# First block of a column sum loaded by two transfers, 16 partitions and then 112, in place of one of 128

## The chip, the cores and the metric

The kernel runs on one core of a Trainium2 chip. The metric is the device time of one execution in microseconds (us), the median over runs.

## The reference

```
x = randn(8192, 8192).astype(float32)
def reference(x): return np.sum(x, axis=0)
```

The input is 268.4 MB, the output 32 KB. Every byte of x has to come into the core once.

## The kernel before

x is cut into 32 blocks of 256 rows. A block lies in SBUF, the core's on-chip memory, as 128 partitions with two rows each, that is 65,536 bytes in one piece per partition. In the trace each such piece is one packet of a DMA engine. Three buffers take turns. The SyncE queue (SP) issues one transfer per block, and VectorE adds two 8192-wide rows at a time into a running sum.

```
P = 128; K = 2; NBUF = 3
xr = x.rearrange("(b p k) c -> b p k c", p=P, k=K)
bufs = [pool.tile([P, K, C], F32, ...) for b in range(NBUF)]
...
def take(sem, n):
    nc.vector.sem_inc(sem, -n)._wait_ge(sem, n)
def block(b):                         # two additions per block
    take(s_buf[b], 17)                # 16 from the transfer, 1 from the block before
    ... tensor_tensor row 0 += carry            (L123)
    nc.vector.sem_inc(s_free, 1)                # the buffer of the block before is free
    ... tensor_tensor row 1 += row 0            (L128)
...
take(s_buf[0], 16)                    # block 0
nc.vector.tensor_tensor(out=rows(0, 1), in0=rows(0, 1), in1=rows(0, 0), op=ADD)   # L134
...
for t in range(last):
    i = nc.sync.dma_start(out=bufs[t % NBUF][:], in_=xr[t])
    if t >= NBUF:
        i._wait_ge(s_free, t - NBUF + 1)
    i.then_inc(s_buf[t % NBUF], 16)
```

The last block comes in six strips of columns. TensorE, with a matrix of ones, sums it and the carry over the partitions; that tail is not touched by the change.

## Time and profile before

| | before |
|---|---|
| time, median of 5 runs beside the change | 627.57 us (627.48 to 627.78) |
| share of the DMA engines' time | 99.2% |
| VectorE busy | 85% |
| rate in the steady part | 434 GB/s |
| first addition on VectorE starts at | 23.16 us |

The page's groups of instructions tell how VectorE stands to the DMA. The columns are: line, engine, operation, output and inputs by name and by shape, count, busy us, mean ns of one, then the idle time before them and what ended it (DVEq L118 is VectorE's own sequencer at the wait in `take`).

```profile
L123 DVE TENSOR_TENSOR buf<-buf,buf 128x8192 f32<-128x8192 f32 x29 | 252.1, 8693 | 58.2 <-DVEq L118 58.2
...
L134 DVE TENSOR_TENSOR buf<-buf 128x8192 f32<-128x8192 f32 x1 | 8.7, 8693 | 23.2 <-DVEq L118 23.2
```

VectorE waits 58.2 us before 29 blocks, 2 us each, and 23.2 us for the first one. It follows the DMA stream. The other views of the kernel before are read in the prediction.

### The profile page before, as it was taken

How to read it: one execution, taken by the hardware profiler on the slowest of the kernel's cores; microseconds unless marked ns; L12 is line 12 of the kernel's file. 1: busy time of each engine (PE TensorE's matmuls, PEld its weight loads, DVE VectorE, ACT ScalarE, POOL GpSimd, SP SyncE). 2: the span in 40 equal slices, each digit the busy share in tenths (PEclk: the TensorE clock that was granted, in tenths of full speed). 3: DMA queues.
4: the chain of work that ended last, by engine and by line, in shares of the span. 5: the costliest groups of instructions: out<-in, count | busy, mean ns of one | idle time of the engine just before them, and what ended most of it. 6: DMA issues, size and time to landing. Idle time of an engine off the chain costs nothing. (4 is left out here: it accounts for less than half of the span.)

```text
span 625.9 us, 576 instructions
## 1 busy us (share of the span) xinstructions
PE 14.2 (2%) x148; PEld 4.5 (1%) x148; DVE 530.8 (85%) x65; ACT 3.7 (1%) x6; POOL 0.3 (0%) x5
## 2 busy tenths in 40 slices
PE   0000000000000000000000000000000000000017
PEld 0000000000000000000000000000000000000002
DVE  0538988889888899888898888988889888899886
ACT  0000000000000000000000000000000000000001
POOL 0000000000000000000000000000000000000000
PEclk9999999999999999999999999999999999999999
DMA  9999999999999999999999999999999999999997
GB/s 402 402 469 402 465 406 465 406 465 406 457 415 436 436 415 457 402 469 402 469 402 469 402 469 402 469 402 465 406 461 410 452 419 431 440 410 461 402 429 312
DMA packets 6141, 268.49 MB, mean 429 GB/s; under 512 B 620, under 2 KB 880, under 8 KB 1404
## 3 DMA queue, kind: packets, MB, share of 16 engines
q1 hardware_dynamic: 6120, 268.47, 99.2%
q8 instruction: 1, 0.02, 0.0%
q10 hardware_dynamic: 20, 0.00, 0.0%
HBM read 268.44 MB, written 0.03 MB: 429 GB/s over the span
## 5 line engine op out<-in xcount | busy, mean ns | idle before, releaser
L123 DVE TENSOR_TENSOR buf<-buf,buf 128x8192 f32<-128x8192 f32 x29 | 252.1, 8693 | 58.2 <-DVEq L118 58.2
L128 DVE TENSOR_TENSOR buf<-buf 128x8192 f32<-128x8192 f32 x29 | 252.1, 8693 | 6.9 <-DVEq L118 6.9
L134 DVE TENSOR_TENSOR buf<-buf 128x8192 f32<-128x8192 f32 x1 | 8.7, 8693 | 23.2 <-DVEq L118 23.2
L85 PE MATMUL ps<-buf,ones 128*32 128x512 f32 (+3 forms) x144 | 12.6, 496 | 608.8 <-DMA buf<-in_x_dram 608.1
L72 DVE TENSOR_TENSOR buf<-buf,buf 128x4096 f32<-128x4096 f32 x2 | 8.8, 4422 | 1.6 <-DMA buf<-in_x_dram 1.6
L72 DVE TENSOR_TENSOR buf<-buf 128x2048 f32<-128x2048 f32 (+1 forms) x3 | 8.9, 3000 | 0.1
L85 PEld LDWEIGHTS ps<-buf,ones 128*32 128x32 f32 x144 | 4.1, 114 | 617.1 <-DMA buf<-in_x_dram 610.6
L209 ACT COPY res<-ps 128x512 f32<-128x512 f32 (+2 forms) x5 | 2.5, 491 | 618.5 <-PE ps L85 618.5
L209 DVE COPY res<-ps 128x64 f32<-128x64 f32 x1 | 0.2, 225 | 2.6 <-PE ps L85 2.6
L100 PE MATMUL ps<-buf,ones 128*32 128x512 f32 x4 | 1.9, 592 | 0.0
L209 ACT ACT_TABLE_LOAD x1 | 1.3, 1283 | 0.9 <-SPq L108 0.9
L100 PEld LDWEIGHTS ps<-buf,ones 128*32 128x32 f32 x4 | 0.4, 110 | 1.3 <-issue 1.3
L109 POOL MEMSET ones<- 128x32 f32 x1 | 0.1, 125 | 0.5 <-SPq L108 0.5
L256 POOL MEMSET const-bfloat16-1.0<- 128x1 bf16 x1 | 0.1, 102 | 0.0
L256 POOL MEMSET const-uint8-127<- 128x1 uint8 x1 | 0.1, 102 | 0.0
L256 POOL MEMSET const-float32-0.0<- 128x1 f32 x1 | 0.1, 99 | 0.2 <-issue 0.2
L256 POOL MEMSET const-float32-1.0<- 128x1 f32 x1 | 0.1, 99 | 0.0
## 6 DMA issues: line engine op xcount, KB each, us to landing
buf<-in_x_dram SPq DMA_DIRECT2D x3, 2048.0 KB, 19.4
buf<-in_x_dram SPq DMA_DIRECT2D x1, 1024.0 KB, 25.5
buf<-in_x_dram SPq DMA_DIRECT2D x1, 768.0 KB, 26.8
buf<-in_x_dram SPq DMA_DIRECT2D x31, 29.7
buf<-in_x_dram SPq DMA_DIRECT2D x1, 256.0 KB, 22.6
out_dram<-res SPq DMA_DIRECT2D x1, 24.0 KB
out_dram<-res SPq DMA_DIRECT2D x1, 4.0 KB
out_dram<-res ACTq DMA_DIRECT2D x1, 4.0 KB
```

Source lines behind the costliest of these rows:

```text
L72: i = nc.vector.tensor_tensor(out=o, in0=a, in1=b, op=ADD)
L85: i = nc.tensor.matmul(out=ps[n][32 * j : 32 * j + 32, 0 : w // NJ], lhsT=ones[:], rhs=runs[:, j], start=start, stop=True, skip_group_chec ...
L100: nc.tensor.matmul(out=ps[len(STRIPS)][0:32, :], lhsT=ones[:], rhs=rows(last, 1, 0, 512), start=True, stop=True,)
L109: nc.gpsimd.memset(ones[:], 1.0).then_inc(s_one, 1)
L123: nc.vector.tensor_tensor(out=r0, in0=r0, in1=bufs[(b - 1) % NBUF][:, 1, :], op=ADD).then_inc(s_op, 1)
L128: nc.vector.tensor_tensor(out=r1, in0=r1, in1=r0, op=ADD).then_inc(s_buf[(b + 1) % NBUF], 1)
L134: nc.vector.tensor_tensor(out=rows(0, 1), in0=rows(0, 1), in1=rows(0, 0), op=ADD).then_inc(s_buf[1], 1)
L209: c = nc.vector.tensor_copy(out=o, in_=p) if n == 5 else nc.scalar.copy(o, p)
L256: nc = _bacc.Bacc("TRN2", target_bir_lowering=False, num_devices=1)
```

## The change

Block 0 gets two transfers. The first has one partition for each of the 16 DMA engines, presumably so that every engine gets its first piece of work sooner. The second has the other 112 partitions. VectorE waits for both.

```diff
-        take(s_buf[0], 16)
+        take(s_buf[0], 32)
...
         for t in range(last):
+            if t == 0:
+                nc.sync.dma_start(out=bufs[0][0:16], in_=xr[0][0:16]).then_inc(
+                    s_buf[0], 16
+                )
+                nc.sync.dma_start(out=bufs[0][16:P], in_=xr[0][16:P]).then_inc(
+                    s_buf[0], 16
+                )
+                continue
             i = nc.sync.dma_start(out=bufs[t % NBUF][:], in_=xr[t])
```

## The prediction

> **What bounds the kernel now.** I read four views, in this order: the page's busy times and slices, its DMA part, the table of busy time by stage, and the timeline of the start. The page says at once which resource is full.
>
> ```profile
> span 625.9 us, 576 instructions
> PE 14.2 (2%) x148; PEld 4.5 (1%) x148; DVE 530.8 (85%) x65; ACT 3.7 (1%) x6; POOL 0.3 (0%) x5
> ...
> DMA  9999999999999999999999999999999999999997
> ...
> q1 hardware_dynamic: 6120, 268.47, 99.2%
> ```
>
> The reader is to see that the 16 DMA engines are busy in every slice (q1 took 99.2% of their time), while VectorE, the busiest compute engine, is at 85%. A kernel that reads 268.4 MB once and has its DMA engines full can only be made shorter before the first byte, after the last one, or by a faster stream. How fast the stream is, the stages show (last two columns: DMA share, GB/s):
>
> ```profile
> 0.00:23.20 23.20, 0.00 (x0) 0.00 (x0) 0.04 (x1) 1.28 (x1) 0.33 (x5) 1.00 0.97 407
> 23.20:42.40 19.20, 0.00 (x0) 0.00 (x0) 8.66 (x1) 0.00 (x0) 0.00 (x0) 1.00 1.01 437
> 42.40:592.40 550.00, 0.00 (x0) 0.00 (x0) 495.48 (x57) 0.00 (x0) 0.00 (x0) 1.00 1.00 434
> ```
>
> 434 GB/s over 550 us is 27.1 GB/s for each of 16 engines. A row of a block is 2 x 8192 x 4 = 65,536 B, one packet, so one packet takes 65,536 / 27.1 = 2.42 us; the packet records in the trace say 2.418. A block of 128 rows is 8 packets on each engine, 19.35 us. The start in half microseconds:
>
> ```profile
> 1.50:2.00 0.50, 0.00 (x0) 0.00 (x0) 0.00 (x0) 0.50 (x1) 0.00 (x0) 1.00 1.15 393
> 2.00:2.50 0.50, 0.00 (x0) 0.00 (x0) 0.00 (x0) 0.19 (x1) 0.00 (x0) 1.00 4.35 1442
> 2.50:3.00 0.50, 0.00 (x0) 0.00 (x0) 0.00 (x0) 0.00 (x0) 0.00 (x0) 1.00 0.75 262
> 3.00:4.50 1.50, 0.00 (x0) 0.00 (x0) 0.00 (x0) 0.00 (x0) 0.00 (x0) 1.00 0.00 0
> ```
>
> A packet is booked whole where it starts, so 393, 1442 and 262 GB/s in half a microsecond are 3, 11 and 2 packets: all 16 engines begin between about 2.0 and 2.65 us, each with one packet. The packet records give 2.9 to 3.4 us for these first ones (0.5 to 1.0 over the normal 2.42) and a spread of 0.65 us between the first and the last engine's start. No engine pauses afterwards. The timeline shows what the start does to VectorE:
>
> ```profile
> 0.97 70.02 SPq L167 DMA_DIRECT2D buf<-in_x_dram  x5
> 23.16 8.69 DVE L134 TENSOR_TENSOR buf<-buf 128x8192 f32<-128x8192 f32 x1 [23.16 <-DVEq L118]
> 42.45 8.69 DVE L123 TENSOR_TENSOR buf<-buf,buf 128x8192 f32<-128x8192 f32 x1 [10.60 <-DVEq L118]
> 51.38 8.69 DVE L128 TENSOR_TENSOR buf<-buf 128x8192 f32<-128x8192 f32 x1 [0.24 <-DVEq L118]
> 61.78 8.69 DVE L123 TENSOR_TENSOR buf<-buf,buf 128x8192 f32<-128x8192 f32 x1 [1.71 <-DVEq L118]
> ```
>
> The queue issues at 0.97 us, block 0 is added at 23.16, and the next two blocks follow 19.3 us apart, the pace of the DMA. VectorE needs 17.4 us a block and waits some 2 us for each. So VectorE would follow a late stream, and would not add to it.
>
> [...]
>
> **The change part by part.** It removes one issue of 8 MB and adds two, of 1 MB and 7 MB. VectorE waits for 32 instead of 16; no arithmetic, buffer or later transfer changes.
> (1) Issue: one more instruction on the queue, 0.33 us by the records of this line (327 to 432 ns). It runs while the first packets move, at 2.9 us or more each. Cost 0.
> (2) Completion: each engine has one more small packet, of 9 ns in the records, some 0.02 us with its gap. Cost 0.02.
> (3) Start, the intent as I read it: the short transfer may be dealt out sooner, so that the last engine need not begin 0.65 us after the first. The most it can save is that spread[...]. I put it at 0.3 us saved.
> (4) [...]
> (5) [...]
> (6) After that. An engine has 248 packets of full rows and then the strips, back to back[...]. The slowest is the last at the end too. A late landing moves VectorE and the later issues with it. Transfers wait in the queue some 10 us (29.7 us median from issue to landing against 19.4 of transfer), so an engine ahead of the others may run dry, but the slowest one does not.
> Sum: 0.02 - 0.3 + 15.3 = +15.0, so 627.5 + 15.0 = 642.5 us.
>
> **The rivals.**
> A, [...]only (1) to (3) act, and the time is 627.2, between 626.8 and 627.7. [...]Chance 0.11.
> B, [...]+7 to +10, so 635 to 637. Chance 0.22.
> C, [...] are consecutive: +12 to +20, 639.5 to 647.5. Chance 0.50.
> D, [...] are dealt in turn, row by row or four by four: [...]+58 us, 685; four by four gives about +39. Chance 0.17.
> A wait that takes the place of another I don't expect: the extra count comes from the transfer that now lands last anyway, and VectorE has its 2 us of slack a block.
>
> **Range and chances.** Two per cent is 12.55 us, so slower begins at 640.05 us, inside C near its lower part. Slower: about 0.8 of C and all of D, 0.57. Faster needs 615, which no path of the start can give, with 2 us before the first byte: 0.01. The rest, A, B and the low part of C, is 0.42. The range 627.0 to 657.0 leaves out D and the better part of nothing else; it is lopsided because a bad dealing of the rows has no near bound.
>
> **What would show it.** Right: packets of the first transfer at 9 to 10 us instead of 3, so few bytes between 3 and 10 us; the first addition at about 38 us instead of 23.16; packets of the second transfer at 2.4 to 7 us, unevenly; the steady 434 GB/s and 2.42 us from block 1 or 2 on; VectorE's 8.69 us per addition the same. Wrong: first packets of about 3 us say [...](A); a first addition at 31 to 33 us says B, after 60 us D. If the start is late by as much as I say but the end is not, the skew between engines was made up, which (6) denies.

The sum of the forecast came to +15.0 us, 642.5 us in all, with a range of 627.0 to 657.0. The 15.3 us in it were the figure for steps (4) and (5), the slower packets of the first and of the second transfer. Both steps, and parts of the rivals, rested on an assumption about which partitions slow each other when they are written at once, and no run had shown it. The rivals: A, the two transfers cost nothing; B and C, block 0 comes late, and in C each engine gets seven consecutive partitions of the 112; D, the 112 rows go out in turn. The figures of B, C and D rest on the same assumption.

## The result

The changed kernel took 649.07 us (median of 5 runs, 648.55 to 649.38), the kernel before 627.57 in the same rounds: 21.5 us more, a ratio of 1.0342 with a 95% interval of 1.0326 to 1.0357. Ratios here are the mean time of one kernel's fast runs over that of the other's of the same rounds, so they are not quite the ratio of the medians quoted.

The page of the changed kernel, its span, busy times, DMA slices and main queue:

```profile
span 647.6 us, 577 instructions
...
PE 14.2 (2%) x148; PEld 4.5 (1%) x148; DVE 530.8 (82%) x65; ACT 3.7 (1%) x6; POOL 0.3 (0%) x5
...
DMA  9999999999999999999999999999999999999986
...
q1 hardware_dynamic: 6136, 268.47, 99.1%
```

No engine has more work: VectorE is busy for 530.8 us as before. The DMA engines look as full as before, and that is the trap of this view: a packet that is slow counts as busy for all of its time. What they moved shows it: in the first stage below the share is 0.96 at 117 GB/s. The table of stages (last two columns: DMA share and GB/s; a packet is booked whole where it starts, so short stages are coarse):

```profile
0.00:9.00 9.00, 0.00 (x0) 0.00 (x0) 0.00 (x0) 1.28 (x1) 0.33 (x5) 1.00 0.96 117
9.00:18.40 9.40, 0.00 (x0) 0.00 (x0) 0.00 (x0) 0.00 (x0) 0.00 (x0) 1.00 1.09 223
18.40:44.00 25.60, 0.00 (x0) 0.00 (x0) 0.00 (x0) 0.00 (x0) 0.00 (x0) 1.00 0.94 241
44.00:60.00 16.00, 0.00 (x0) 0.00 (x0) 8.69 (x1) 0.00 (x0) 0.00 (x0) 1.00 1.05 455
60.00:610.00 550.00, 0.00 (x0) 0.00 (x0) 491.50 (x57) 0.00 (x0) 0.00 (x0) 1.00 1.00 433
```

For 44 us the stream runs at about a quarter, then about half of its rate; from the second block on it is what it was, 433 GB/s. The start, closer:

```profile
2.00:2.50 0.50, 0.00 (x0) 0.00 (x0) 0.00 (x0) 0.19 (x1) 0.00 (x0) 1.00 14.16 1704
2.50:3.00 0.50, 0.00 (x0) 0.00 (x0) 0.00 (x0) 0.00 (x0) 0.00 (x0) 1.00 3.11 393
3.00:4.50 1.50, 0.00 (x0) 0.00 (x0) 0.00 (x0) 0.00 (x0) 0.00 (x0) 1.00 0.00 0
...
10.00:11.00 1.00, 0.00 (x0) 0.00 (x0) 0.00 (x0) 0.00 (x0) 0.00 (x0) 1.00 2.14 393
11.00:12.00 1.00, 0.00 (x0) 0.00 (x0) 0.00 (x0) 0.00 (x0) 0.00 (x0) 1.00 2.99 590
```

13 and 3 packets start before 3 us, and most of the engines take up their second one only after 10 us. Before, all 16 second packets (699 GB/s in 1.5 us) started between 4.5 and 6 us:

```profile
4.50:6.00 1.50, 0.00 (x0) 0.00 (x0) 0.00 (x0) 0.00 (x0) 0.00 (x0) 1.00 1.61 699
```

The timeline of SP and VectorE in the changed kernel:

```profile
0.96 0.40 SPq L169 DMA_DIRECT2D buf<-in_x_dram  x1
1.43 0.40 SPq L172 DMA_DIRECT2D buf<-in_x_dram  x1
...
45.30 8.69 DVE L134 TENSOR_TENSOR buf<-buf 128x8192 f32<-128x8192 f32 x1 [45.30 <-DVEq L118]
64.58 8.69 DVE L123 TENSOR_TENSOR buf<-buf,buf 128x8192 f32<-128x8192 f32 x1 [10.58 <-DVEq L118]
```

The first addition starts at 45.30 us, 22.1 later than before; the next follows at the old distance of 19.3. And the groups:

```profile
L123 DVE TENSOR_TENSOR buf<-buf,buf 128x8192 f32<-128x8192 f32 x29 | 252.1, 8693 | 57.8 <-DVEq L118 57.8
...
L134 DVE TENSOR_TENSOR buf<-buf 128x8192 f32<-128x8192 f32 x1 | 8.7, 8693 | 45.3 <-DVEq L118 45.3
```

The whole loss is in the one wait for block 0; the other 29 waits are unchanged. So the question is only why block 0 takes 22 us longer to land.

The packet records answer it by the step. The records don't name the engine, but within 0.03 us of the end of each packet another one starts, so they can be strung into 16 rows of 248 packets, one for each engine. The mean of all first, all second packets and so on, in us:

| | 1st | 2nd | 3rd | 4th | 5th | 6th | 7th | 8th |
|---|---|---|---|---|---|---|---|---|
| before | 3.13 | 2.42 | 2.42 | 2.42 | 2.42 | 2.42 | 2.42 | 2.42 |
| changed | 8.63 | 5.47 | 4.76 | 3.33 | 3.84 | 4.64 | 4.76 | 4.61 |

The first column is the transfer of 16 partitions, the other seven are the 112. I had expected the first column. I had not expected that the others would be slow on nearly all engines alike (the third packets took 4.74 to 4.86 us, the seventh 4.72 to 4.83).

### The profile page after: what moved, and what is told of

Read it like the earlier page. It is cut to its first block, busy times and chain, and to the rows that moved or that the text cites. A ratio compares the mean times of both kernels' runs of the same rounds, so it can differ in the third digit from the quotient of the medians.

```text
span 647.6 us, 577 instructions
## 1 busy us (share of the span) xinstructions
PE 14.2 (2%) x148; PEld 4.5 (1%) x148; DVE 530.8 (82%) x65; ACT 3.7 (1%) x6; POOL 0.3 (0%) x5
## 5 line engine op out<-in xcount | busy, mean ns | idle before, releaser
L123 DVE TENSOR_TENSOR buf<-buf,buf 128x8192 f32<-128x8192 f32 x29 | 252.1, 8693 | 57.8 <-DVEq L118 57.8
L85 PEld LDWEIGHTS ps<-buf,ones 128*32 128x32 f32 x144 | 4.1, 115 | 638.8 <-DMA buf<-in_x_dram 632.3
```

What stands on the lines that cost most here:

```text
L85: i = nc.tensor.matmul(out=ps[n][32 * j : 32 * j + 32, 0 : w // NJ], lhsT=ones[:], rhs=runs[:, j], start=start, stop=True, skip_group_chec ...
L123: nc.vector.tensor_tensor(out=r0, in0=r0, in1=bufs[(b - 1) % NBUF][:, 1, :], op=ADD).then_inc(s_op, 1)
```

## The experiments

A step is here one row on each of the 16 engines. The theory: some rows of a step slow each other (they collide), and which ones do depends on the partitions they go to. Rivals: it is the reading of 16 neighbouring rows that is slow, not the writing; two transfers, or many, cost something as such; the 112 rows go in some other way than seven consecutive partitions to an engine, that is, in steps of 16 partitions seven apart.

### Two transfers that both keep all 128 partitions (cols)

Block 0 is cut by columns in place of partitions, with the first piece again 1 MB.

```diff
+            if t == 0:
+                for to in (slice(0, 2048), slice(2048, 16384)):
+                    nc.sync.dma_start(
+                        out=bufs[0].rearrange("p k c -> p (k c)")[:, to],
+                        in_=xr[0].rearrange("p k c -> p (k c)")[:, to],
+                    ).then_inc(s_buf[0], 16)
+                continue
```

> Block 0 again in two transfers, the first again 1 MB, but cut by columns: all 128 partitions, 8,192 B of each, then the other 57,344 B of each. [...]627.5 us, within 0.5, first addition at 23 to 23.5 us. If two transfers as such cost something (rival: a second issue, a second completion, a restart of the stream), it comes out at several us more, up to the 649 of the change. If a short first transfer brings the start forward as the change intended, 627.0 to 627.3.

Measured: 628.06 us (628.03 to 628.27) beside 627.78, ratio 1.0005, interval 0.9991 to 1.0019. Two transfers cost nothing as such. Nor do they gain anything, though the timeline shows a first addition earlier than the 23 to 23.5 us expected:

```profile
22.57 8.69 DVE L134 TENSOR_TENSOR buf<-buf 128x8192 f32<-128x8192 f32 x1 [22.57 <-DVEq L118]
42.23 8.69 DVE L123 TENSOR_TENSOR buf<-buf,buf 128x8192 f32<-128x8192 f32 x1 [10.97 <-DVEq L118]
...
61.97 8.69 DVE L123 TENSOR_TENSOR buf<-buf,buf 128x8192 f32<-128x8192 f32 x1 [2.11 <-DVEq L118]
```

Block 0 is added 0.59 us earlier than before (22.57 against 23.16), block 1 0.22 earlier (42.45 before), block 2 0.19 later (61.78). The lead is gone within two blocks. Why it goes, no run here shows.

### The first transfer by itself, to three sets of partitions (p4, p8, p16)

An extra 1 MB is loaded ahead of everything into the third buffer, always from the same 16 rows. Block 2 overwrites it later, so the result stays right; its issue waits, on a semaphore of its own (s_probe), until the extra load has landed.

```diff
+        for to, fr in (
+            (slice(0, 16), slice(0, 16)),
+        ):
+            nc.sync.dma_start(out=bufs[2][to], in_=xr[0][fr]).then_inc(s_probe, 16)
         for t in range(last):
             i = nc.sync.dma_start(out=bufs[t % NBUF][:], in_=xr[t])
+            if t == 2:
+                i._wait_ge(s_probe, 16)
```

That is p4. The other two differ in the destination alone:

```diff
-            (slice(0, 16), slice(0, 16)),
+            (slice(0, 61, 4), slice(0, 16)),      # p8: partitions 0, 4, ... 60
+            (slice(32, 93, 4), slice(0, 16)),     # p16: partitions 32, 36, ... 92
```

> The kernel before, with one extra transfer of 1 MB put ahead of everything: rows 0 to 15 of the block to partitions 0 to 15 of the third buffer, which block 2 overwrites later. It measures the first transfer of the change by itself; the same 1 MB at the full rate is 2.4 us. [...]8.5 to 9.7 us, so 636 to 637.2 us. Rival (reading 16 neighbouring rows is slow, whatever the destination): the same here, but then the same in p8 and p16 too. Rival (no such effect, all loss is in the second transfer): 630.

> As p4, the same 16 source rows, to partitions 0, 4, ... 60: [...]632.3 us (within 0.5), packets of 4.5 to 5.3 us. Rival of the source: as p4. No effect: 630.

> As p4, the same 16 source rows, to partitions 32, 36, ... 92: [...]2.42 us, so 629.9 us (within 0.5), packets of about 3 us as in the kernel before. Rival of the source: as p4, 636 or more.

| | to partitions | time, us | over 627.78 |
|---|---|---|---|
| p4 | 0, 1, ... 15 | 636.58 | 8.80 |
| p8 (two fast runs) | 0, 4, ... 60 | 632.33 and 632.36 | 4.6 |
| p16 | 32, 36, ... 92 | 630.22 | 2.44 |

The same bytes from the same rows cost 8.8, 4.6 or 2.4 us, by nothing but the numbers of the partitions they go to. These differences are under 2% of the time, but the fast runs of the three kernels lie apart: 636.50 to 636.72, 632.33 to 632.36, 630.07 to 630.91 us. The reading side falls as a cause. In p4 the engines wait as in the changed kernel: 16 packets start by 3 us, and the 16 second ones (350 GB/s in 3 us) only between 9 and 12 us. The stages at the start:

```profile
1.50:3.00 1.50, 0.00 (x0) 0.00 (x0) 0.00 (x0) 0.69 (x1) 0.00 (x0) 1.00 5.73 699
...
9.00:12.00 3.00, 0.00 (x0) 0.00 (x0) 0.00 (x0) 0.00 (x0) 0.00 (x0) 1.00 1.26 350
12.00:15.00 3.00, 0.00 (x0) 0.00 (x0) 0.00 (x0) 0.00 (x0) 0.00 (x0) 1.00 0.81 350
```

In p16 all 16 second packets (699 GB/s in 1.5 us is 16 packets) start within 4.5 to 6 us:

```profile
4.50:6.00 1.50, 0.00 (x0) 0.00 (x0) 0.00 (x0) 0.00 (x0) 0.00 (x0) 1.00 1.62 699
```

Two of p8's four runs, the profiled one among them, took 707.9 us, with every packet at 2.71 us in place of 2.42 from the start to the end (387 GB/s in place of 434 between 100 and 600 us). The same program took 632.3 us in its other two runs, so this is not the effect of the extra transfer; both runs are left out. It also means that no fast profile of p8 exists: its time is known, its packets in the fast state are not.

### The same partitions from rows far apart (p4src)

```diff
-            (slice(0, 16), slice(0, 16)),
+            (slice(0, 16), slice(0, 121, 8)),     # to 0..15, from rows 0, 8, ... 120
```

> As p4, partitions 0 to 15 again, but from source rows 0, 8, ... 120 of the block instead of 16 neighbouring rows. [...]the same as p4, within 0.5 us. Rival of the source: clearly less than p4.

Measured: 636.37 us beside 627.84, 8.5 us more; p4 had 8.8 more. Where the rows are read from changes next to nothing.

### The second transfer by itself (p112)

```diff
-            (slice(0, 16), slice(0, 16)),
+            (slice(16, 128), slice(16, 128)),
```

> The change's second transfer by itself, as an extra load of partitions 16 to 127 ahead of the unchanged block 0. Its bytes at the full rate are 7 x 2.42 = 16.9 us. From the change's own trace (7 packets of 30 to 33 us in all, then 0.8 more in the next) it should add some 31 us, so 658.5 us within 2; 14 us of it are loss. [...]

Measured: 658.44 us beside 627.84, 30.6 us more. At the full rate seven packets are 7 x 2.42 = 16.9, so 13.7 us are lost here, without the transfer of 16 ahead of it. The estimate from the change's trace (31 us) fits. If it were slow only because of the transfer of 16 ahead of it, it would have added 17 to 20 us; that possibility falls.

### The dealing written out (deal7, deal16)

Block 0 in eight transfers of 16 partitions: in deal7 the first with 16 neighbours and seven more with 16 partitions seven apart, in deal16 with 16 neighbours each time. VectorE waits for all eight. Each kernel has one of the two `for` lines.

```diff
-        take(s_buf[0], 16)
+        take(s_buf[0], 128)
...
+            if t == 0:
+                for to in (slice(0, 16), slice(16, 122, 7), slice(17, 123, 7), ... slice(22, 128, 7)):  # deal7
+                for to in (slice(0, 16), slice(16, 32), slice(32, 48), ... slice(112, 128)):            # deal16
+                    nc.sync.dma_start(out=bufs[0][to], in_=xr[0][to]).then_inc(s_buf[0], 16)
+                continue
```

> Block 0 with the dealing written out: partitions 0 to 15 first, as in the change, then seven transfers of 16 partitions each, 16, 23, 30 ... 121, then 17, 24, ... 122, and so on[...]. If the chip deals the 112 rows of the change in this way (theory), the time and the pattern of packets are those of the change: 649 us within 1. If it deals them otherwise, the time differs from 649 by more. [...]

> Block 0 in eight transfers of 16 neighbouring partitions: [...]8 steps of 9.2 to 9.7 us instead of 19.35, so +54 to +58 us, 682 to 686 us. If the chip's dealing of the 112 were row by row, the change would have had this time; it had 649, so this only measures the other end of the scale. Rival (each further transfer costs a fixed time of its own, 20 us or so[...]): near to deal7, which has as many transfers of the same size.

deal7 took 648.59 us, ratio 1.0327 (1.0310 to 1.0345): the time of the change. Its packets too are those of the change, step by step: 8.48, 5.49, 4.77, 3.13, 3.79, 4.60, 4.63, 4.49 us. So the change's second transfer goes like deal7's seven, in steps of 16 partitions seven apart, or in some way that cannot be told from it here. deal16, with as many transfers of the same size, took 681.14 us, 53.3 over the kernel before, 0.9 less than the 682 to 686 expected, with packets of 8.43 us at the first step and 9.12 at every later one. Two stages, of deal7 and then of deal16; the changed kernel had 223 and 241 GB/s in them:

```profile
9.00:18.40 9.40, 0.00 (x0) 0.00 (x0) 0.00 (x0) 0.00 (x0) 0.00 (x0) 1.00 1.10 223
18.40:44.00 25.60, 0.00 (x0) 0.00 (x0) 0.00 (x0) 0.00 (x0) 0.00 (x0) 1.00 0.93 246
...
9.00:18.40 9.40, 0.00 (x0) 0.00 (x0) 0.00 (x0) 0.00 (x0) 0.00 (x0) 1.00 0.98 112
18.40:44.00 25.60, 0.00 (x0) 0.00 (x0) 0.00 (x0) 0.00 (x0) 0.00 (x0) 1.00 1.07 123
```

The number of transfers is not the cost; which partitions meet in a step is.

The steps of the change's second transfer took 5.47, 4.76, 3.33, 3.84, 4.64, 4.76, 4.61 us. In the third of them two engines took 4.79 and 4.80 us, as if they shared the rate of one (2 x 2.42 = 4.84, an estimate), and the other 14 took 2.97 to 3.46; in the fourth 14 engines took 3.70 to 3.90. In the other five all 16 took 4.4 us or more. That made a new question: do a few engines that collide hold up the others?

### One partition of p16 exchanged, and two (p15x4, q_14x4)

Four extra transfers of 16 partitions, step 4, from 28, 29, 30 and 31 on (p15x4) or from 24, 25, 26 and 27 on (q_14x4). The first of p15x4 has the partitions of p16 with 28 in place of 92, that of q_14x4 has 24 and 28 in place of 88 and 92. In the expectations from here on, (a) is that only the engines that collide are slow, (b) that the others are held up too.

```diff
-            (slice(0, 16), slice(0, 16)),
+            (slice(28, 89, 4), slice(0, 16)), (slice(29, 90, 4), slice(16, 32)),     # p15x4
+            (slice(30, 91, 4), slice(32, 48)), (slice(31, 92, 4), slice(48, 64)),
+            (slice(24, 85, 4), slice(0, 16)), (slice(25, 86, 4), slice(16, 32)),     # q_14x4
+            (slice(26, 87, 4), slice(32, 48)), (slice(27, 88, 4), slice(48, 64)),
-                i._wait_ge(s_probe, 16)
+                i._wait_ge(s_probe, 64)
```

> Four extra transfers of 16 rows ahead of everything, to partitions 28, 32, ... 88, then 29, 33, ... and so on: [...](a): 14 engines take 2.42 us a packet from the second on (3 for the first), two take 4.8; the slowest are 4 x 4.84 = 19.4 us later, so 645 to 647 us. [...](b): the other 14 take 3 us or more a packet too, with the same end. The time does not tell them apart, the packet records do.

> As p15x4, four extra transfers of 16 rows, to partitions 24, 28, ... 84 and so on: [...](b): packets of some 4.75 us on all 16, and the end 4 x 2.4 + 9.5 = 19 us late, 647 us. [...](a): 12 engines keep 2.42 us as in p15x4[...], so 652 to 655 us.

p15x4 took 654.30 us, 26.5 over 627.84. Two engines collide and the others are free: of the 64 extra packets, the 56 of the other engines took 2.42 to 3.4 us, the first four of the two colliding engines 4.6 to 5.1, and their last four 7.4 to 8.3. The stages of its start:

```profile
4.50:6.20 1.70, 0.00 (x0) 0.00 (x0) 0.00 (x0) 0.00 (x0) 0.00 (x0) 1.00 1.27 540
6.20:7.20 1.00, 0.00 (x0) 0.00 (x0) 0.00 (x0) 0.00 (x0) 0.00 (x0) 1.00 0.32 66
```

The second packets of all 14 other engines (540 x 1.7 / 65.5) start by 6.2 us, and the first of the two colliding engines follows in the next stage. My time for it was wrong, 645 to 647: I had 4.8 us for all packets of the two. The last four fall in the time when other engines have come to block 0, some 10 us after the first packet; that one of these joins the two, so that three collide, is my estimate (3 x 2.42 = 7.3 us against 7.4 to 8.3) and is not shown. From there until the two are done, 26 us after the first packet, 13 engines took 3.01 to 3.27 us a packet, no longer 2.42.

q_14x4 took 647.60 us, 19.8 over 627.84, as (b) had it. All 16 engines took 5.1 to 5.2 us a packet from the second on:

```profile
4.50:6.00 1.50, 0.00 (x0) 0.00 (x0) 0.00 (x0) 0.00 (x0) 0.00 (x0) 1.00 0.00 0
6.00:8.00 2.00, 0.00 (x0) 0.00 (x0) 0.00 (x0) 0.00 (x0) 0.00 (x0) 1.00 2.62 524
```

No second packet starts before 6 us, and all 16 (524 x 2 / 65.5) start by 8. The source rows are those of p15x4; only the partitions differ. With one partition exchanged two engines took 4.6 to 5.1 us and left the other 14 alone at first; with two exchanged all 16 were slow. How many of the 16 collide themselves in q_14x4, the records don't show. The change's own two quick steps were less clean than p15x4: in the third most of the other engines took 3.0 to 3.2 us, in the fourth 3.7 to 3.9. The engines don't pass from step to step at one moment (the second packets start between 9 and 12 us), so collisions of two steps may overlap; that this is why is not shown.

### The first step of seven alone, and another sixteen partitions seven apart (q_step7, q_cross)

```diff
-            (slice(0, 16), slice(0, 16)),
+            (slice(16, 122, 7), slice(0, 16)),    # q_step7: partitions 16, 23, ... 121
+            (slice(11, 117, 7), slice(0, 16)),    # q_cross: partitions 11, 18, ... 116
```

For q_cross, (a) is that the step runs like that of p16, (b) that it is slow all the same.

> The first step of the seven in deal7 by itself, as an extra transfer: partitions 16, 23, ... 121[...]. (a) [...]12 packets of 2.4 to 3.2 us and 4 of 4.8 or more. (b) all wait: 16 packets of 4.5 us or more. The time, 632 to 634 us, is set by the slowest engine in both.

> As p16, but to partitions 11, 18, 25, ... 116: [...](a): packets of 2.4 to 3.2 us and 630 us, as p16. [...](b): packets of 4 us and more, 631.5 us or more. It decides whether (b) can be why in the change's second transfer nearly every packet took 4.75 us[...].

q_step7 took 632.16 us beside 627.84, and all 16 packets 4.1 to 5.2 us: (b). Its second packets start after 6 us, 11 of them by 7.5 and five by 9:

```profile
4.50:6.00 1.50, 0.00 (x0) 0.00 (x0) 0.00 (x0) 0.00 (x0) 0.00 (x0) 1.00 0.00 0
6.00:7.50 1.50, 0.00 (x0) 0.00 (x0) 0.00 (x0) 0.00 (x0) 0.00 (x0) 1.00 1.37 481
7.50:9.00 1.50, 0.00 (x0) 0.00 (x0) 0.00 (x0) 0.00 (x0) 0.00 (x0) 1.00 0.58 218
```

q_cross took 630.57, 2.7 more, with first packets of 2.43 to 3.25 us:

```profile
4.50:6.00 1.50, 0.00 (x0) 0.00 (x0) 0.00 (x0) 0.00 (x0) 0.00 (x0) 1.00 1.64 699
```

As in p16, all second packets start within 4.5 to 6 us. Sixteen partitions seven apart are not slow as such: from 11 on they cost 2.7 us, next to the 2.4 of p16, and from 16 on 4.3. So the slow steps of the second transfer come from which partitions meet in them, and they can slow all 16 engines alike.

## Why the prediction was right, and where it was off

**The direction and the place of the loss held.** The loss comes in block 0 from the partitions that are written at once, it is paid before block 1, and it stays to the end: 22.1 us at the first addition, 21.7 in the span. Of the rivals, A (only (1) to (3) act) falls with p4 against p16, 8.8 us against 2.4; B (635 to 637 us) falls with the measured 649.07, and D (dealt in turn) with deal7, which matches the change, and deal16, which is 32 us above it. C's dealing stands as far as deal7 can tell; its time, 639.5 to 647.5, was 1.6 us short of the measured 649.07. That the range up to 657.0 held is in part luck: the sum was 642.5 us, the range was widened upwards for a bad dealing of the rows, and the dealing was the likely one; what filled the gap was an effect that the prediction does not have.

**Steps (1) and (2)**, issue and completion: the two issues took 0.40 us each and lie ahead of packets of 8.63 us. cols, with as many transfers, costs nothing that can be measured. Right.

**Step (3)**, 0.3 us saved at the start: wrong, though small. The last engine starts its first packet 0.78 us after the first one, against 0.65 before. One packet per engine did not bring the start forward. In cols the spread was 0.45 and the first addition came 0.59 earlier, but the end did not.

**Step (4)**, the first transfer: measured 636.58 - 630.22 = 6.4 us (p4 less p16). Sixteen neighbouring partitions took 9.12 us a packet in deal16, 3.8 times the 2.42 of the kernel before.

**Step (5)**, the second transfer: the step that failed in size. The forecast had 15.3 us for (4) and (5) together; the runs give 6.4 and, by p112, 13.7. The dealing fits (deal7). What failed is that I reckoned with some engines slow and the others free: in q_14x4 and q_step7 all 16 engines took 5.1 to 5.2 and 4.1 to 5.2 us a packet in place of 2.42, and in five of the seven steps of the change all took 4.4 us or more. So the expected unevenness did not come: in the trace all engines end block 0 between 39.3 and 42.1 us after its start, and the first addition starts at 45.30 us, not at about 38. The sum from the parts is then 6.4 + 13.7 = 20.1 of the 21.5 us. The missing 1.4 are not settled; the change's first step after the 16 partitions took 5.47 us against 4.70 in p112, so part of it lies in that passage.

**Step (6)**, no catching up: right. Additions follow at 19.3 us from the second on, the two engines that took 4.8 us in the third step of the seven still end their full rows last, at 624.0 and 624.2 us against 622.0 to 622.9 for the others, and the waits before the other 29 blocks are 57.8 us against 58.2.

What stays open is which partitions collide and why, and where the other engines are held when some do. The runs show that all 16 are slow with two partitions of p16 exchanged (q_14x4, 5.2 us a packet), not at first with one (p15x4, 2.42 to 3.4 for 14 of them), and that neither the rows read (p4src; q_14x4 against p15x4) nor the distance of seven (q_cross) is the cause. Why the others were held up less in the later part of p15x4 (3.0 us a packet) than in q_14x4 (5.2) is open too.

## What to carry to other kernels

When a kernel is full on its DMA engines, cut a transfer by columns and keep all 128 partitions in each piece (cols: no measurable cost, ratio 1.0005): cutting it by partitions can let partitions meet that slow each other, and here that slowed down all 16 engines (5.2 us a packet in q_14x4 in place of 2.42). A slice of 16 neighbouring partitions, 0 to 15, cost 8.8 us where the same megabyte to 32, 36, ... 92 cost 2.4. A DMA share of 99% told nothing here, so look at the GB/s of each stage and at the length of single packets.
